# Order of loads, transposes and squares at the start of a hybrid decoder layer, with the pools of its last phase and the branch rows reordered

## The chip, the cores and the metric

The kernel runs on one NeuronCore of a Trainium2 chip. Its engines are TensorE (PE in the profile, with weight loads as PEld), VectorE (DVE), ScalarE (ACT), GpSimd (POOL) and SyncE (SP), which issues most of the transfers. The metric is the time of one execution on the device in microseconds; the profile belongs to one further execution.

## The reference

One layer of a decoder trunk is computed in float32 for a prompt of 1024 rows and for eight samples of 8 rows, together 1088 rows of width 1024. The weights are shared.

```
mod = silu(c) @ ada_w + ada_b;  shift, scale, gate = split(mod, 3)
h = rmsnorm(x, norm_g) * (1 + scale) + shift
z = h @ w_in + b_in                       # split into the inputs of A, B, C and the gates m_g
ya = chunk_gmlp(...)   * silu(a_g)        # A: mixing matrices over 128 positions
yb = swa_branch(...)   * silu(b_g)        # B: attention with a window of 128
yc = mlstm_branch(...) * silu(c_g)        # C: causal conv on q/k, matrix memory
merged = sum over branches of sigmoid(m_g) * (y @ w_branch)
x_out = x + gate * (merged @ w_out)
```

## The kernel before

Float32 products are made of three fast matmuls: each operand is split into a high part (rounded by a cast on ACT or DVE) and a low part (a subtraction on DVE), and high x high, high x low and low x high are added in one bank of PSUM. The rows stand in the free dimension, in three chunks `CH` of 384, 384 and 320 columns for `h` transposed, or in nine row tiles of 128 (the last has 64) for products by rows.

**The start** (up to about 87 us) loads x in nine tiles `xt` (x0 to x8), computes the modulation and makes `h` transposed, split into `hh[k]` and `hlo[k]` for k = 0 to 7. While it does so, the first weight slab is multiplied with it. `LOADS` gives the order of the transfers on SP: `x` a tile of x, `r` small rows, `a0` to `a3` the four parts of the modulation weights (four transfers of 512 KB each), `w0`, `w1` the halves of slab 0, `s` small rows. `STEPS` gives the order of the work, and inside it PE, ACT, DVE and POOL each keep that order (`manual_schedule`, line 451). The steps are:

- `Qn` (`squares`): ACT squares tile n and sums its rows; two small operations on POOL make the reciprocal root. `Nn` (`norm`): DVE scales tile n by it.
- `Tk c` (`x_keep`): PE transposes piece k of the chunk's three tiles into a bank of the pool `pss` (three banks, `pk`), and DVE or ACT copies it to SBUF. `place` puts the pieces into `xT0`, the first of the two slab buffers, and then into the slots m0, m1, ... of x tiles that are done.
- `Aj` (`mod_a`): 32 matmuls of modulation part j, and a copy on ACT. `Bj` (`mod_b`): eight small matmuls and four small operations on DVE, which leave scale and shift for k = 2j and 2j + 1.
- `Wi` (`slab0_split`): two casts on ACT, two subtractions on DVE. `Hk c` (`hprep`): ACT applies scale and shift, DVE makes the high and the low part, from the kept piece or, where `T` was not called, straight from the transposes in PSUM. `Gk c i` (`part`): three matmuls of slab half i with the piece, or six without i. `S`, `P` and `X` are small rows, the splitting of slab 1, and pads.

**The middle** (to about 598 us) goes through slabs 1 to 16, which alternate between the two buffers `hl` of the pool `wts`, and computes the conv, the matrix memory, the attention and the inner products of branch A. Outside the start a planner decides each engine's and queue's order by its own idea of when things are ready.

**The last phase** runs over a list of `items`. Each item has weights to prepare (`raw_load` on SP into one of five tiles `raw2`, `w_split` on ACT and DVE into a tile `prod`) and products of 288 and 256 columns (`CUT`). The first ones are the gate products of branch A; then come, for each branch, `gate_pair` and `proj`, where `proj` multiplies the branch's rows `yh`, `yl` by `w_branch` (`lastev` and the rest of `run`, lines 1698 to 1719). The rows of the second and third branch come from DRAM by `y_load`, whose item stands four items ahead of the branch's first `proj`. It goes through one tile `stage` with two halves:

```
for f in range(4):
    y_tiles(f)
    for b in range(2):
        c = slice(HT * b, HT * b + HT)
        x = stage[0][:, b]
        nc.sync.dma_start(x, dy[0 if br == 2 else 1, f, :, c])
        S.copy(yh[f][:, c], x)
        V.tensor_tensor(yl[f][:, c], x, yh[f][:, c].bitcast(F32), ALU.subtract)
```

`run` of `proj` multiplies the first 544 columns (h = 0) with k = 0 to 3 before the second 544.

The pools of the last phase lie where the pools `wts` and `gtmp` lay: first `e2` (14,336 bytes a partition: results and rows), then `w3` (6,144: sums of weights), then `w2` (10,240 for the five raw tiles and 24,576 for the six `prod`). In `wts` the two slab buffers have 16,896 bytes each.

Of the kernel before, what the change touches and what calls it, by code (L numbers as in the profile page):

```python
# [8 lines left out]
F32 = mybir.dt.float32  # L9
# [18 lines left out]
HT = NT // 2  # L28
HC = HT // 2
CUT = ((0, 288), (288, 256))  # L30
LEAD = 5
LOADS = "x0 r x1 x2 a0 x3 x4 x5 w0 x6 x7 x8 w1 a1 a2 a3 s"

STEPS = """Q0 N0 Q1 N1 Q2 N2
T20 T30 T40 A0 T50 T60 T70 Q3 B0 H00 H10 N3 Q4 N4 Q5 N5 W0
H01 H11 T21 T31 G000 G100 T41 T51 G010 G110 T61 T71 Q6 N6 Q7 N7 W1 Q8 N8
H02 H12 T22 G001 G101 T32 G011 G111 T42 T52 G020 T62 G120 T72 G021 G121
A1 B1 H20 H30 H21 H31 G20 G30 H22 G21 H32 G31 A2 G22 B2 G32 H40 H50 H41 H51 G40 G50 H42 G41 H52 A3 G51
B3 G42 H60 G52 H70 H61 H71 G60 H62 S G70 H72 P G61 G71 G62 G72 X"""


@with_exitstack
def trunk_kernel(ctx: ExitStack, tc: tile.TileContext, I, O):
    nc = tc.nc
    V, S, G, T = nc.vector, nc.scalar, nc.gpsimd, nc.tensor
# [32 lines left out]
    def slot(tag, shape, dt=F32, name=None):  # L78
        return sp.tile(shape, dt, tag=tag, name=name or tag)
# [16 lines left out]
    def kv(ap):  # L96
        return ap.rearrange("(k p) c -> p k c", p=128)
# [143 lines left out]
    with tc.tile_pool(name="start", bufs=1, side="right", reuse_waits="tile") as st:  # L241
# [47 lines left out]

        for step in LOADS.split():  # L290
            if step == "r":
# [82 lines left out]
        def place(n):  # L374
            if not places:
                places.append([xT0.rearrange("p a c -> p (a c)"), 0])
            if places[-1][1] + n > places[-1][0].shape[1]:
                places.append([slot(f"m{len(places) - 1}", [128, 1152], name="xT"), 0])
            p = places[-1]
            p[1] += n  # L380
            return p[0][:, p[1] - n:p[1]]

        def x_transpose(k, ci):
            px = pk()
            for i in range(3):
                t0, tn = TILES[3 * ci + i]
                tr(px[:, 128 * i:128 * i + tn], xt[3 * ci + i][:tn, 128 * k:128 * k + 128])
            return px

        def x_keep(k, ci):  # L390
            n = CH[ci][1]
            px = x_transpose(k, ci)
            kept_x[k, ci] = place(n)
            if k % 3:
                V.tensor_copy(kept_x[k, ci], px[:, :n])
            else:
                S.copy(kept_x[k, ci], px[:, :n])
# [37 lines left out]
        def start_step(step):  # L435
            d = [int(x) for x in step[1:]]
            if step == "P":
                load_pieces(1, [None] * 3 + [st.tile([128, 528], F32, name="raw1")])
            elif step == "S":
                ps = pk()  # L440
                tr(ps[:, 0:68], R1)
                V.tensor_copy(cols[:, 0:CADA], ps[:, 0:CADA])
                V.tensor_copy(cols[:, CCB:100], ps[:, CADA:68])
            elif step[0] == "G":
                for i in d[2:] or range(2):
                    part(d[0], d[1], i)
            else:
                {"Q": squares, "N": norm, "W": slab0_split, "A": mod_a, "B": mod_b, "T": x_keep, "H": hprep, "X": pads}[step[0]](*d)

        ET = mybir.EngineType  # L450
        with tc.manual_schedule(engines={ET.PE, ET.Activation, ET.DVE, ET.Pool}):
            for step in STEPS.split():
                start_step(step)
# [22 lines left out]
    with tc.tile_pool(name="cph", bufs=1, side="right", reuse_waits="tile") as c1:  # L476
# [303 lines left out]
        for h in range(1, 4):  # L780
            hl = next_slab()
            for s in range(2):
                f = 4 * s + h
# [616 lines left out]
    one.close()  # L1400


    e2 = ctx.enter_context(tc.tile_pool(name="e2", bufs=1, reuse_waits="tile"))
    w3 = ctx.enter_context(tc.tile_pool(name="w3", bufs=1, reuse_waits="tile"))
    w2 = ctx.enter_context(tc.tile_pool(name="w2", bufs=1, reuse_waits="tile"))
    banks = [0]

    def bank():
# [12 lines left out]
    newest = [None]  # L1421

    def raw_load(src):
        r = w2.tile([128, 512], F32, tag="raw", bufs=5, name="raw2")
        newest[0] = nc.sync.dma_start(r.rearrange("p (k c) -> p k c", k=src.shape[1]), src).ins
        return r

# [5 lines left out]
    def w_split(x, tile=None):  # L1433
        t = tile if tile is not None else w2.tile([128, 2, 512], F32R, tag="prod", bufs=6, name="prod")
        a = S.copy(t[:, 0], x)  # L1435
        b = V.tensor_tensor(t[:, 1], x, t[:, 0].bitcast(F32), ALU.subtract)  # L1436
        splits.append((a.ins, b.ins))
        return t
# [22 lines left out]
    def seven(cols2, order, final):  # L1461
# [4 lines left out]
        def loads():  # L1466
            for i, c in enumerate(cols2):
                w = kv(w_in[:, c:c + 128])
                for j in range(2):
                    st["a", i, j] = raw_load(w[:, 4 * j:4 * j + 4])  # L1470
# [95 lines left out]
    def plain(cols2, final):  # L1566

        st = {}

        def prep(i, j):  # L1570
            if not i and not j:
                return first[0]
            return w_split(raw_load(kv(w_in[:, cols2[i]:cols2[i] + 128])[:, 4 * j:4 * j + 4]))

        def run(i, h):
            for j in range(2):
                c = part_(h, j)
                ps = bank()[:, :CUT[j][1]]
                for k in range(8):
                    three(ps, st[i, k // 4], k % 4, hh[k][:, c], hlo[k][:, c], k == 0, k == 7)  # L1580
                x = tt(j)
                with tc.high_priority():
                    S.copy(x, ps)
                final(i, h, j, x)

        def have(i, j, t):
            st[i, j] = t
            if j:
                run(i, 1)

        out = [(lambda i=i, j=j: prep(i, j), lambda t, i=i, j=j: have(i, j, t)) for i in range(2) for j in range(2)]
        return out + [(None, lambda _, i=i: run(i, 0)) for i in range(2)]

    Q7 = (1, 6, 7, 5, 3, 2, 4)
# [29 lines left out]
    def y_tiles(f):  # L1624
        yh[f] = y2[0].tile([128, NT], F32R, tag=f"yh{f}", name="yh")
        yl[f] = slot(("y2", "y3", "y7")[f - 1], [128, NT], F32R, name="yl") if f else y2[0].tile([128, NT], F32R, tag="yl0", name="yl")
# [39 lines left out]
    def y_load(n):  # L1666
        br = ORDER_BR[n]
        if not stage:
            stage.append(slot("m5", [128, 2, HT], name="stage"))
        for f in range(4):  # L1670
            y_tiles(f)
            for b in range(2):
                c = slice(HT * b, HT * b + HT)
                x = stage[0][:, b]
                nc.sync.dma_start(x, dy[0 if br == 2 else 1, f, :, c])
                S.copy(yh[f][:, c], x)  # L1676
                V.tensor_tensor(yl[f][:, c], x, yh[f][:, c].bitcast(F32), ALU.subtract)
# [14 lines left out]
    def proj(n, f, Tt):  # L1692
        br = ORDER_BR[n]

        def prep():
            return w_split(raw_load(kv(I["w_branch_" + "abc"[br]][0][:, 128 * f:128 * f + 128])))

        def run(t):
            if n == 2 and f % 4 == 3:
                m_tiles(f)  # L1700
            for h in range(2):
                for j in range(2):
                    c = part_(h, j)
                    x = Tt[f, h, j]
                    ps = bank()[:, :CUT[j][1]]
                    for k in range(4):
                        three(ps, t, k, yh[k][:, c], yl[k][:, c], k == 0, k == 3)
                    prev = None
                    if n:
                        prev = mp(CUT[j][1], "mprev")  # L1710
                        lastm[0] = nc.sync.dma_start(prev, dmg[f, :, c]).ins
                    with tc.high_priority():
                        lastev[0] = V.scalar_tensor_tensor(x, x, 1.0, ps, ALU.add, ALU.mult).ins
                    if n:
                        V.tensor_tensor(x, x, prev, ALU.add)
                    if n == 2 and f % 4 == 3:
                        m_split(f, c.start, CUT[j][1], x)
                    else:
                        nc.sync.dma_start(dmg[f, :, c], x)

        items.append((prep, run))
# [106 lines left out]
    def wo_load(i):  # L1828
        for j in range(4):
            t = None  # L1830
            if SLOTS[i]:
                t = slot(SLOTS[i][j], [128, 1040], F32R, name="wo")[:, 16:1040].rearrange("p (a c) -> p a c", a=2)
            a = KS8[2 * j]
            src = kv(w_out[:, 256 * i:256 * i + 256])
            r = w2.tile([128, 512], F32, tag="raw", bufs=5, name="raw2")
            for u in range(2):
                nc.sync.dma_start(r[:, 256 * u:256 * u + 256], src[:, KS8[2 * j + u]])
            wo[i, j] = w_split(r, t)

    wo_load(0)  # L1840
    for i in range(4):
# [3 lines left out]
        c = slice(256 * i, 256 * i + 256)  # L1845
        for n in tuple(range(9)) if i < 3 else (8,) + tuple(range(8)):
# [4 lines left out]
            for z in range(8):  # L1851
                w, k = wo[i, z // 2], KS8[z]
# [50 lines left out]
```

## Time and profile before

| what | value |
|---|---|
| median of 3 runs | 1199.02 us (1198.87 to 1199.79) |
| profiled execution | 1201.82 us, span of its instructions 1200.1 us |
| PE busy | 1161.1 us, 97% of the span |
| DVE busy | 789.1 us, 66% |
| ACT busy | 490.2 us, 41% |
| POOL busy | 76.2 us, 6% |
| mean granted PE clock | 0.987 of full |

Busy time counts an instruction from its start to its end; matmuls overlap in the pipeline, so the pitch of a group says more than one's duration. "Idle before" is the time an engine stood still ahead of an instruction, with what ended it. The granted clock (PEclk) is a share of TensorE's full clock; 0.50 is its lower level. A window's row gives the stretch, its length, the busy time of PE, PEld, DVE, ACT and POOL in this order (with the number of instructions), PEclk, the busy share of the DMA engines and GB/s.

### The profile page before, as it was taken

What the parts mean: (1) busy time and instruction counts of PE and PEld (TensorE: products, weight loads), DVE (VectorE), ACT (ScalarE), POOL (GpSimd) and SP (SyncE); (2) the same over time, 40 slices, a digit from 0 to 9 for tenths busy, and PEclk for the clock granted to TensorE, in tenths of its full rate; (3) what the DMA queues carried; (4) which work ended last, traced back from release to release, by engine and by line L of the source; (5) the groups of instructions that cost most, each with busy time, mean ns of one, the idle gap of its engine ahead of it and who ended that gap; (6) DMA issues with size and microseconds to landing.
All of it is one profiled execution on the core that took longest, in us unless ns stands there. A gap on an engine that the chain in (4) does not pass through costs nothing.

```text
span 1200.1 us, 23137 instructions
## 1 busy us (share of the span) xinstructions
PE 1161.1 (97%) x8924; PEld 1115.8 (93%) x8924; DVE 789.1 (66%) x1862; ACT 490.2 (41%) x1233; POOL 76.2 (6%) x109
## 2 busy tenths in 40 slices
PE   4799999999999999999999999999999999999998
PEld 3589999999999998988998999999899999999998
DVE  4468768664549578886588975555666676668433
ACT  4343454543333367887354442223333342235100
POOL 2100002010114101020000000000000000000000
PEclk8799999999999999999999999999899999999999
DMA  9702223131323211122144225444533354455422
GB/s 299 241 23 77 73 63 109 31 106 64 109 65 94 61 33 58 54 67 78 40 133 143 63 72 161 145 131 143 166 110 110 110 169 128 128 183 187 135 90 74
DMA packets 150773, 129.74 MB, mean 108 GB/s; under 512 B 13613, under 2 KB 140213, under 8 KB 150648
## 3 DMA queue, kind: packets, MB, share of 16 engines
q1 hardware_dynamic: 142984, 118.96, 33.7%
q0 software_dynamic: 2240, 7.08, 1.7%
q10 hardware_dynamic: 5440, 2.23, 0.7%
q8 instruction: 70, 1.15, 0.4%
q14 instruction: 39, 0.32, 0.1%
HBM read 99.39 MB, written 29.82 MB: 108 GB/s over the span
## 4 chain that ended last, share of the span: by engine, by line
PE 85%; DVE 7%; DMA 3%; ACT 2%; issue 1%; POOL 0%; SPq 0%; DVEq 0%; ACTq 0%; POOLq 0%
PE pg L89 45%; PE pk L89 24%; PE pu L89 13%; PE pk L93 2%; DMA stage<-dy 1%; DVE hl L129 1%; DVE acc L494 1%; PE pu L93 1%; DMA raw<-in_w_in_dram 1%; DMA xt<-in_x_prompt_dram 0%; DVE vv L535 0%; DMA Cs<-in_state_mlstm_C_dram 0%; ACT junk L332 0%; DMA E<-scr 0%; DMA dy<-stage 0%
## 5 line engine op out<-in xcount | busy, mean ns | idle before, releaser
L89 PE MATMUL pg<-hl,hl 128*128 128x256 f32 (+3 forms) x904 | 277.9, 308 | 0.5 <-DVE hl L414 0.3
L89 PE MATMUL pg<-hh,hl 128*128 128x384 f32 (+1 forms) x912 | 238.7, 336 | 2.7 <-DVE hh L413 2.7
L89 PE MATMUL pg<-hl,hh 128*128 128x256 f32 (+1 forms) x1008 | 177.2, 283 | 0.2 <-DVE zif L539 0.2
L89 PEld LDWEIGHTS pg<-hl,hl 128*128 128x128 f32 x904 | 171.1, 189 | 2.0 <-DVE hl L414 1.2
L89 PEld LDWEIGHTS pg<-hh,hl 128*128 128x128 f32 x912 | 163.1, 190 | 5.8 <-DVE hh L413 3.5
L89 PEld LDWEIGHTS pg<-hl,hh 128*128 128x128 f32 x1008 | 150.4, 188 | 0.7 <-PE pg L89 0.4
L1435 ACT CAST prod<-raw 128x512 fp32r<-128x512 f32 x76 | 47.0, 620 | 127.9 <-PE pk L89 55.7
L89 PE MATMUL pg<-hh,prod 128*128 128x288 f32 (+1 forms) x400 | 84.0, 290 | 2.3 <-ACT prod L1435 2.1
L89 PE MATMUL pk<-hh,prod 128*128 128x256 f32 (+1 forms) x384 | 78.3, 285 | 0.0
L1436 DVE TENSOR_TENSOR prod<-raw,prod 128x512 fp32r<-128x512 f32 x76 | 52.0, 687 | 29.4 <-ACT prod L1435 29.1
L89 PEld LDWEIGHTS pg<-hh,prod 128*128 128x128 f32 x400 | 65.8, 188 | 3.2 <-ACT prod L1435 2.3
L1435 ACT CAST prod<-comb 128x512 fp32r<-128x512 f32 x60 | 36.9, 616 | 68.8 <-PE pk L89 30.9
L1599 ACT ACTIVATE tt<-tt,bh 128x288 f32<-128x288 f32 x96 | 49.9, 522 | 36.9 <-DVE tt L1561 14.2
L89 PEld LDWEIGHTS pk<-hh,prod 128*128 128x128 f32 x384 | 62.9, 189 | 0.8 <-DVE hl L840 0.4
L89 PE MATMUL pg<-yh,prod 128*128 128x288 f32 (+1 forms) x288 | 61.9, 293 | 0.0
L89 PE MATMUL pk<-yh,prod 128*128 128x256 f32 (+1 forms) x288 | 59.4, 286 | 2.3 <-ACT yh L1676 2.3
L89 PE MATMUL pg<-hl,prod 128*128 128x288 f32 (+1 forms) x200 | 57.7, 289 | 0.0
L89 PE MATMUL pk<-tc,prod 128*128 128x256 f32 (+1 forms) x408 | 56.3, 287 | 0.0
L89 PE MATMUL pu<-hh,prod 128*128 128x288 f32 (+1 forms) x272 | 56.3, 287 | 0.0
L89 PE MATMUL pg<-tc,prod 128*128 128x288 f32 (+1 forms) x396 | 55.8, 290 | 0.0
L89 PE MATMUL pk<-hl,prod 128*128 128x256 f32 (+1 forms) x192 | 54.7, 285 | 0.0
L89 PEld LDWEIGHTS pk<-tc,prod 128*128 128x128 f32 x408 | 52.7, 188 | 1.3 <-issue 1.3
(542 smaller groups left out, 2657.6 us busy)
## 6 DMA issues: line engine op xcount, KB each, us to landing
raw<-in_w_in_dram SPq DMA_DIRECT2D x124, 256.0 KB
adaraw<-in_ada_w_dram SPq DMA_DIRECT2D x16, 512.0 KB
stage<-dy SPq DMA_DIRECT2D x24, 272.0 KB
dmg<-tt SPq DMA_DIRECT2D x44, 144.0 KB
dmg<-tt SPq DMA_DIRECT2D x44, 128.0 KB
mprev<-dmg SPq DMA_DIRECT2D x32, 144.0 KB
xt<-in_x_prompt_dram SPq DMA_DIRECT2D x8, 512.0 KB
graw<-in_ada_w_dram SPq DMA_DIRECT2D x16, 256.0 KB
```

Of the source, the lines that this page charges most:

```text
L89: T.matmul(out, lhsT=lhsT, rhs=rhs, start=start, stop=stop)
L93: T.transpose(out, in_, ident[:k, :k])
L129: V.tensor_tensor(hl[:, 1, off:off + m], raw[:, :m], hl[:, 0, off:off + m].bitcast(F32), ALU.subtract)
L494: V.scalar_tensor_tensor(acc, xp[:, j:j + XC], cwcol[:, 8 * j + f:8 * j + f + 1], acc, ALU.mult, ALU.add)
L1435: a = S.copy(t[:, 0], x)
L1436: b = V.tensor_tensor(t[:, 1], x, t[:, 0].bitcast(F32), ALU.subtract)
L1599: S.activation(x, x, AF.Tanh, bias=bh[:, b:b + 1], scale=0.5)
```

## The change

The nine x tiles are loaded before all modulation weights and slab halves. `STEPS` is written anew: all 24 transposed pieces are kept (18 before), all of them are made before the first `H`, squares stand about one tile ahead of the scaling, and each pair A, B stands between the products of the pair before. In the last third of the columns the kept pieces alternate between ACT and DVE. The raw tiles get a pool of their own, `w2r`, and the pools of the last phase are opened as w2r, w3, e2, w2. `y_load` claims all four tiles first and then goes through the four tiles for the first half of the columns and then for the second.

```diff
--- before.py
+++ after.py
@@ -29,14 +29,13 @@
 HC = HT // 2
 CUT = ((0, 288), (288, 256))
 LEAD = 5
-LOADS = "x0 r x1 x2 a0 x3 x4 x5 w0 x6 x7 x8 w1 a1 a2 a3 s"
-
-STEPS = """Q0 N0 Q1 N1 Q2 N2
-T20 T30 T40 A0 T50 T60 T70 Q3 B0 H00 H10 N3 Q4 N4 Q5 N5 W0
-H01 H11 T21 T31 G000 G100 T41 T51 G010 G110 T61 T71 Q6 N6 Q7 N7 W1 Q8 N8
-H02 H12 T22 G001 G101 T32 G011 G111 T42 T52 G020 T62 G120 T72 G021 G121
-A1 B1 H20 H30 H21 H31 G20 G30 H22 G21 H32 G31 A2 G22 B2 G32 H40 H50 H41 H51 G40 G50 H42 G41 H52 A3 G51
-B3 G42 H60 G52 H70 H61 H71 G60 H62 S G70 H72 P G61 G71 G62 G72 X"""
+LOADS = "x0 r x1 x2 x3 x4 x5 x6 x7 x8 a0 w0 a1 w1 a2 a3 s"
+
+STEPS = """Q0 N0 Q1 N1 Q2 N2 Q3 T00 T10 T20 Q4 N3 T30 T40 Q5 T50 N4 T60 T70
+Q6 N5 T01 T11 Q7 N6 T21 T31 T41 Q8 N7 T51 T61 N8 T71 T02 T12 T22 A0 T32 T42 W0 T52 T62 B0 T72
+H00 H10 G000 H01 G100 H11 G010 H02 G110 H12 A1 G020 G120 B1 W1 G001 G101 G011 H20 G111 H30 G021 H21 G121
+H31 G20 H22 G30 H32 A2 G21 B2 G31 G22 H40 H50 G32 H41 H51 G40 H42 G50 H52 G41 A3 G51 B3 G42
+H60 H70 G52 H61 H71 G60 H62 S G70 H72 G61 P G71 G62 G72 X"""
 
 
 @with_exitstack
@@ -391,7 +390,7 @@
             n = CH[ci][1]
             px = x_transpose(k, ci)
             kept_x[k, ci] = place(n)
-            if k % 3:
+            if k % (2 if ci == 2 else 3):
                 V.tensor_copy(kept_x[k, ci], px[:, :n])
             else:
                 S.copy(kept_x[k, ci], px[:, :n])
@@ -1400,9 +1399,7 @@
     one.close()
 
 
-    e2 = ctx.enter_context(tc.tile_pool(name="e2", bufs=1, reuse_waits="tile"))
-    w3 = ctx.enter_context(tc.tile_pool(name="w3", bufs=1, reuse_waits="tile"))
-    w2 = ctx.enter_context(tc.tile_pool(name="w2", bufs=1, reuse_waits="tile"))
+    w2r, w3, e2, w2 = (ctx.enter_context(tc.tile_pool(name=n, bufs=1, reuse_waits="tile")) for n in ("w2r", "w3", "e2", "w2"))
     banks = [0]
 
     def bank():
@@ -1421,7 +1418,7 @@
     newest = [None]
 
     def raw_load(src):
-        r = w2.tile([128, 512], F32, tag="raw", bufs=5, name="raw2")
+        r = w2r.tile([128, 512], F32, tag="raw", bufs=5, name="raw2")
         newest[0] = nc.sync.dma_start(r.rearrange("p (k c) -> p k c", k=src.shape[1]), src).ins
         return r
 
@@ -1669,8 +1666,9 @@
             stage.append(slot("m5", [128, 2, HT], name="stage"))
         for f in range(4):
             y_tiles(f)
-            for b in range(2):
-                c = slice(HT * b, HT * b + HT)
+        for b in range(2):
+            c = slice(HT * b, HT * b + HT)
+            for f in range(4):
                 x = stage[0][:, b]
                 nc.sync.dma_start(x, dy[0 if br == 2 else 1, f, :, c])
                 S.copy(yh[f][:, c], x)
@@ -1832,7 +1830,7 @@
                 t = slot(SLOTS[i][j], [128, 1040], F32R, name="wo")[:, 16:1040].rearrange("p (a c) -> p a c", a=2)
             a = KS8[2 * j]
             src = kv(w_out[:, 256 * i:256 * i + 256])
-            r = w2.tile([128, 512], F32, tag="raw", bufs=5, name="raw2")
+            r = w2r.tile([128, 512], F32, tag="raw", bufs=5, name="raw2")
             for u in range(2):
                 nc.sync.dma_start(r[:, 256 * u:256 * u + 256], src[:, KS8[2 * j + u]])
             wo[i, j] = w_split(r, t)
```

## Rows read from the trace of the kernel before

**Rows 1.** Windows of the start: length, busy us per engine, PEclk, DMA share, GB/s.
```profile
12.30:40.00 27.70, 16.26 (x102) 12.14 (x102) 15.83 (x36) 13.59 (x25) 6.29 (x12) 0.83 1.09 339
40.00:56.90 16.90, 14.55 (x87) 10.62 (x87) 6.57 (x21) 3.75 (x7) 0.00 (x0) 0.78 0.69 218
56.90:87.00 30.10, 27.95 (x197) 23.90 (x198) 20.27 (x68) 13.43 (x25) 0.00 (x0) 0.94 0.01 3
```

**Rows 2.** Waits of PE, 0 to 87 us: total us, times, longest.
```profile
PE pk L93 <- DVE xt L337: 14.1, 8, 3.1
```

**Rows 3.** Timeline of PE near 600 us: start, us, instruction, idle before.
```profile
601.73 0.40 PE L89 MATMUL pg<-hh,prod 128*128 128x288 f32 x1 [2.08 <-ACT prod L1435]
```

**Rows 4.** Timeline of SP's queue, 597 to 602 us.
```profile
597.99 2.58 SPq L1425 DMA_DIRECT2D raw<-in_w_in_dram  x5
```

**Rows 5.** Timeline of PE, near 850 us.
```profile
853.30 0.61 PE L89 MATMUL pk<-yh,prod 128*128 128x288 f32 x1 [2.33 <-ACT yh L1676]
```

**Rows 6.** Windows behind these two waits.
```profile
602.46:608.00 5.54, 5.54 (x32) 5.54 (x33) 4.16 (x7) 2.62 (x6) 0.54 (x1) 0.69 0.97 271
853.30:860.00 6.70, 6.54 (x28) 6.22 (x29) 3.40 (x7) 1.41 (x3) 0.00 (x0) 0.52 0.35 106
```

**Rows 7.** Chain that ended last, 0 to 120 us: start, us, what.
```profile
9.29 1.16 ACT junk L332 x2
...
10.90 0.56 POOL rstd L167
11.48 0.77 DVE xt L337
...
17.21 1.28 PE pk L93 x9
...
23.50 0.94 POOL rstd L167
...
42.18 2.22 PE pg L89 x6
...
62.24 0.52 PE pg L89 x3
...
63.29 1.86 PE pk L89 x32
...
75.97 0.81 PE pk L89 x8
```

**Rows 8.** Timeline of DVE, 37 to 62 us.
```profile
37.46 1.29 DVE L288 TENSOR_TENSOR hl<-raw,hl 128x512 fp32r<-128x512 f32 x2
...
56.46 0.36 DVE L413 CAST hh<-hf 128x384 fp32r<-128x384 f32 x1 [0.45 <-ACT hf L407]
...
57.33 0.35 DVE L413 CAST hh<-hf 128x384 fp32r<-128x384 f32 x1
...
59.92 0.22 DVE L410 TENSOR_TENSOR hf<-xT,modA 128x64 f32<-128x64 f32 x1
...
61.27 0.22 DVE L410 TENSOR_TENSOR hf<-xT,modA 128x64 f32<-128x64 f32 x1
```

**Rows 9.** Timeline of PE, last matmul of the start's steps.
```profile
86.72 0.30 PE L89 MATMUL pk<-hh,hl 128*128 128x320 f32 x1
```

**Rows 10.** Timeline of SP's queue, 818 to 862 us.
```profile
830.87 0.42 SPq L1675 DMA_DIRECT2D stage<-dy  x1
...
832.59 0.32 SPq L1675 DMA_DIRECT2D stage<-dy  x1
...
846.74 0.32 SPq L1675 DMA_DIRECT2D stage<-dy  x1
...
848.34 6.02 SPq L1675 DMA_DIRECT2D stage<-dy  x3
```

**Rows 11.** Timeline of ACT, 846 to 862 us.
```profile
849.66 0.65 ACT L1676 CAST yh<-stage 128x544 fp32r<-128x544 f32 x1 [1.40 <-DMA stage<-dy]
...
852.61 0.65 ACT L1676 CAST yh<-stage 128x544 fp32r<-128x544 f32 x1 [0.54 <-DMA stage<-dy]
```

## The prediction

> **What bounds the kernel now.** I began with the table of busy time: TensorE (PE) is busy 97% of the span, so an edit counts only if it gives PE back time in which it waits, or in which its clock is low. Then I looked where those 3% lie. The windows of the first 87 us [rows 1] show PE busy 16.3 of 27.7 us and 14.6 of 16.9, at granted clocks of 0.83 and 0.78, then 28.0 of 30.1 at 0.94. Look also at DMA in them: full (share 1.09, 339 GB/s) until 40 us, next to nothing after 57. The waits say for whom PE stood: 14.1 us in eight waits for a scaled x tile [rows 2]. From that I read the cause: modulation weights (a0, 2 MB) and the slab's w0 are queued between x2 and x6, so the squares of x3 to x8 come late, and the engines run in the written order of steps, so PE can't go on with other work.
>
> Behind the start there are two more places. PE waits 2.08 us, to 601.73, for the first product weights of the last phase [rows 3]: SP sent their raw loads only at 597.99 [rows 4]. It waits 2.33 us, to 853.30, for yh [rows 5]. Behind each the granted clock is low for a while: mean 0.69 over 5.54 us, 0.52 over 6.70 us [rows 6].
>
> **The start, step by step.** No arithmetic is removed. Six more transposed pieces are copied to SBUF (24 where it was 18; k = 0 and 1 were read from PSUM before). PE does the same 24 transposes, 48 matmul groups (one step G has one or two) and four pairs A, B. The loads are the same bytes and the same issues in another order, so the queue's end is unmoved. A tile is 512 KiB, 1.5 us at 339 GB/s [rows 1]; x2 is there by 9.3, as its square starts then [rows 7]; x3 to x7 follow by 16.8, the half tile x8 by 17.5. Four loads of 0.5 MB (a0) take 6 us and w0 1.5: a0 23.5, w0 25, a1 31, w1 32.5, a2 38.5, a3 44.5.
>
> ACT: a square takes 1.16 [rows 7]. After Q2 (10.45) come six squares, 7.0 us, five copies between them at some 0.45 (estimate: DVE's 384-column copy bounds it, inside a pitch of 0.87 for two operations [rows 8]), 2.2, and waits for the first transposes and for DVE's scalings, about 2.2: Q8 ends at 21.9, after its tile has come, so ACT and not DMA sets this. From a square's end to the scaling it was 1.0 (10.45 to 11.48) [rows 7]; one POOL step took 0.94 instead of 0.56 when DVE scaled beside it, and here N7 does run beside Q8's: 1.4, then 0.77 for N8: 24.1.
>
> By this row one POOL step is 0.4 longer, and that is in the 24.1. The Trainium skill, "SBUF — State Buffer", section "Who interferes with whom", goes further: GpSimd and VectorE in some of its operations take a shared port in turn, and the second waits in full. By it both of POOL's steps could each stand behind a scaling of 0.77, which is 1.1 more than by the row: the start would save 15.9 and not the 17.0 below. The rows show one step held, not two, so I stay with them.
>
> Then PE: three transposes for each piece, 1.28 for nine [rows 7], so 0.43. T02, T12, T22 1.3; A0 1.86 at the high clock, 2.6 taken, as PE has been half idle; T32 to T62 1.7; B0 0.81, 1.1 taken; its four small operations on DVE 0.65 (estimate); H00 0.66 on ACT (estimate: a little over a DVE operation on the same piece) and 0.4 for DVE's cast [rows 8]. W0 (1.29 on DVE [rows 8]) falls beside the transposes. Sum 8.4: first G at 32.5. The written order of before comes to its first G behind fewer transposes and no x3; here the change loses some us.
>
> From there PE has everything it needs close by. A group of three 384-column matmuls takes 0.52 at the high clock (2.4 GHz) and 1.11 at the low (1.2 GHz; 2.22 for two) [rows 7]; with 320 columns 0.44, by the share of the columns. 32 x 0.52 + 16 x 0.44 = 23.7. A1 to A3 3 x 1.86 = 5.6, B1 to B3 3 x 0.81 = 2.4, S 0.4: 32.1 us. On top: the first groups at the low clock, about 2.5 (four groups at 1.11 - 0.52 = 0.59 more); G001 behind W1, whose subtraction (1.29) stands on DVE behind B1's scalings, 1.3; small waits on H in the first pair, 1.2. Sum 5. Last G: 32.5 + 32.1 + 5 = 69.6, against 87.0 now [rows 9]. Is DVE in front? Each H costs it 0.87 (start to start of two casts), 1.35 for the last third [rows 8]: 3.09 per k, 24.7 for eight, with W1, three B's and S 28.3, so 60.8 without waits: PE decides. A1 (36.6), A2 (47) and A3 (57) start behind their loads (31, 38.5, 44.5). The copy of the six extra pieces, about 1.4 on each of ACT and DVE, stands in that 24.1; H reads SBUF at the same 0.87.
>
> Saving 17.4, less 0.4 (estimate) of the next product that now runs inside the last G's: 17.0. Bounds: if all 5 us of losses vanish and A0 runs at 1.86, 23; if G starts 3 us later and two pairs run at the low clock, 7.
>
> What follows (slab 1's split, the conv, the token products) is ordered as before and moves as a whole; its loads are asked for when buffers come free, so they move along.
>
> **The pools.** By my sum over the pools' sizes the raw loads of the last phase lay 20 to 30 KB above the bottom of the space that the slabs leave, in the second slab buffer, which the last slab holds to the end. Now they lie at the bottom, in the first buffer, which holds the slab before it. So the five loads can go while PE still works on the last slab, and split and cast come before PE runs dry (601.73 - 2.08 = 599.65). Saved: 2.08, and the low clock behind it, 5.54 x 0.31 = 1.7: 3.8. Bounds: 0, if the bottom is held as long; 3.8. I take 3.8, the upper end: SP has five loads waiting there that nothing else in the code holds back, and it starts them 1.66 before PE runs dry, which fits a buffer held by PE's last slab. The other pools only change neighbours.
>
> **Branch rows by halves.** Each branch takes eight loads through two stage halves. Written by halves, four loads in a row use one stage half, each behind the subtraction of the one before. If SP kept that order, the second half would start only behind the fourth load. But SP's order isn't the code's: the row of 848.34 holds three, of which, counting from 830.87, only one is this branch's eighth [rows 10]; the other two belong to the next branch and went by 854.4, before this branch's products were done. A load whose stage half is free goes out, so the two chains should still interleave as now (830.87, 832.59 [rows 10]). Does it help then? PE, free at 850.97, started at 853.30, just behind the cast of 852.61, by its place the last tile's other half; the cast of the half that it reads, at 849.66, was over by 850.31 [rows 11]. So the wait goes by the whole tile here, and halves in order give nothing: I take 0. Bounds: minus 2.33 + 6.70 x 0.48 = 5.5 (wait and low clock gone), plus what the serial rival costs.
>
> **Sum.** 17.0 + 3.8 = 20.8. Span 1200.1 to 1179.3, the profiled execution's 1201.8 to 1181.0. The median of the runs is 2.8 below the profiled one, and I move it by the same: 1199.0 to **1178.2 us**.
>
> **Rivals.** (a) The yh wait goes as well: 1178.2 - 5.5 = 1172.7. For it: the first half's four loads stand first wherever engines choose. Against: the whole-tile wait.
> (b) The wait at 599.65 stays: 1182.0. For it: I inferred the addresses; no row shows them. Against: the 597.99 above.
> (c) The start stays at the low clock through k = 0 and 1: twelve groups, 8 x 0.59 + 4 x 0.5 = 6.7, and A1 1.3 more, 8 together: 1186.2. For it: groups are fed at 0.87 or slower in the first pair, so PE has holes; 0.83 and 0.78 in [rows 1]. Against: at the low clock a group (1.11) is longer than DVE's 0.87, so it has no holes there. The Trainium skill, "TensorE: Matmul & The Clock Gate", section "HAM oscillation — how this bites in real kernels", warns of just this: gaps between bursts bring the half clock back. The 0.52 behind the yh wait agrees: a wait of 2.33 was followed by it.
> (d) Slower: SP keeps the written order of the branch loads. A turn is (846.74 - 830.87) / 3 = 5.29 us [rows 10]. The second half's fourth load would go at 846.74 + 0.4 + 3 x 5.29 = 863.0, be landed and cast 3.57 later (846.74 to 850.31) at 866.6 instead of 853.3: 13.3 us, in two branches 26.6: 1204.8. It decides once both together cost over 20.8. Against: SP's reordering above; the second branch also has slack now.
> (e) The order of the start gains nothing because something I don't see comes late: about 1195 to 1199.
>
> **How the numbers follow.** Forecast 0.58; (a) 0.13; (b) 0.09; (c) 0.12; (d) 0.05; (e) 0.03. A measurement tells some 0.2% (2.4 us) from no change. Faster 0.93, same 0.02, slower 0.05. From (a) with 3 us of a better start to (c) with 3 us of a worse one: 1169 to 1189; outside lie (d), (e) and bad ends of the start's bound, under 2 in 10.
>
> **What would show it.** Right: the squares end near 22 us; first G near 32.5, last near 70; PE clock full from about 45 us; no wait for xt after 25 us; raw loads of the last phase sent before 598 and no wait on the first products. The yh wait tells (a) from the forecast, and SP's order of the eight loads tells (d). Wrong: last G after 80 us, PE waiting there for modulation weights or H; new waits of several us at the branch loads.

## The result and the profile after

The changed kernel takes 1185.04 us, the median of 1184.53, 1185.04 and 1186.71; a fourth run took 1608.58 at a mean granted clock of 0.656 and is not compared (with it the median would be 1185.88). The kernel before took 1199.4 beside it, 1198.87 to 1201.35. The ratio is 0.988 with an interval of 0.986 to 0.990: faster, by some 14 us where 20.8 were forecast, inside the range. The profiled execution took 1185.04, its span is 1183.3, 16.8 shorter than before's.

Windows of the start in the trace after (columns as in [rows 1]):

```profile
12.00:28.00 16.00, 11.97 (x75) 9.46 (x79) 10.53 (x19) 9.90 (x20) 7.02 (x14) 0.89 1.09 327
28.00:36.00 8.00, 5.61 (x41) 3.52 (x33) 4.22 (x17) 3.62 (x8) 0.00 (x0) 0.84 1.11 337
36.00:40.00 4.00, 4.00 (x12) 3.55 (x12) 3.73 (x11) 2.25 (x5) 0.00 (x0) 0.50 1.10 348
40.00:46.00 6.00, 5.00 (x52) 3.45 (x51) 4.40 (x12) 2.95 (x6) 0.00 (x0) 0.98 0.86 272
46.00:75.00 29.00, 28.18 (x216) 24.91 (x215) 21.13 (x72) 13.84 (x26) 0.00 (x0) 1.00 0.24 77
```

From 46 us on PE is busy 28.18 of 29 us at the full clock. The holes of [rows 1] now nearly all lie ahead of 46 us: in the first 36 us, 1.0 us just ahead of 45.56, and, at the low clock, the first products. The waits of PE in the same trace:

```profile
PE pk L92 <- DVE xt L336: 8.0, 5, 2.4
PE pk L88 <- ACT yh L1674: 3.3, 1, 3.3
PE pk L88 <- DVE cols L360: 1.5, 1, 1.5
PE pg L88 <- DVE hl L287: 1.0, 1, 1.0
PE pk L92 <- DVE xts L336: 0.8, 1, 0.8
```

The 14.1 us for x [rows 2] are 8.0, none of them past 20 us; the wait for the last, half tile (`xts`), 0.8 where it was 1.9, ends at 25.57. The wait for a small copy on DVE (`cols`) has grown to 1.5 from 0.6, and the 1.0 for slab 0's second half is new. Where they stand is in the timeline of PE after, from modulation part A0 on (the last line answers to [rows 9]):

```profile
26.92 1.93 PE L88 MATMUL pk<-adaraw,sT 128*32 128x256 f32 x32
...
31.07 0.24 PE L92 MATMUL pk<-ident,Ra 32*128 32x32 f32 x1
32.86 1.41 PE L88 MATMUL pk<-sel,msb 128*128 128x9 f32 x8 [1.54 <-DVE cols L360]
...
35.93 0.69 PE L88 MATMUL pg<-hh,hl 128*128 128x384 f32 x1 [0.85 <-DVE hh L412]
...
74.32 0.31 PE L88 MATMUL pk<-hh,hl 128*128 128x320 f32 x1
```

The start's last matmul starts at 74.32 and not at 86.72: 12.4 us earlier. What DVE did ahead of that copy, in its timeline:

```profile
31.01 1.29 DVE L287 TENSOR_TENSOR hl<-raw,hl 128x512 fp32r<-128x512 f32 x2 [1.06 <-ACT hl L286]
32.22 0.48 DVE L394 COPY xT<-pk 128x320 f32<-128x320 f32 x1
32.62 0.18 DVE L360 COPY cols<-pk 128x32 f32<-128x32 f32 x1
```

W0's subtraction (1.29) and the copy of T52 stand in front of it, and all of PE's next steps behind it.

In the last phase, SP's queue (it answers to [rows 4]) and the first products of PE (to [rows 3]):

```profile
551.55 36.79 SPq L1422 DMA_DIRECT2D raw<-in_w_in_dram  x7
```

```profile
586.66 0.40 PE L88 MATMUL pg<-hh,prod 128*128 128x288 f32 x1
...
587.39 0.53 PE L88 MATMUL pg<-hh,prod 128*128 128x288 f32 x2 [0.20 <-DVE prod L1433]
```

The raw loads begin 35 us ahead of the first product, and the fifth of them goes 18 us ahead of it (568.95). The wait of 2.08 is gone; a wait of 0.20 for DVE behind the first two matmuls was there before as well. The last product of the last slab stands 12.98 us earlier than before (584.67 for 597.65), one behind the boundary 16.68 (591.56 for 608.24): 3.7 us come from here. At the branch rows PE and ACT show (as [rows 5] and [rows 11]):

```profile
837.59 0.40 PE L88 MATMUL pk<-yh,prod 128*128 128x288 f32 x1 [3.28 <-ACT yh L1674]
```

```profile
834.08 0.64 ACT L1674 CAST yh<-stage 128x544 fp32r<-128x544 f32 x1 [2.19 <-DMA stage<-dy]
...
836.89 0.65 ACT L1674 CAST yh<-stage 128x544 fp32r<-128x544 f32 x1 [0.41 <-DMA stage<-dy]
```

The wait is there as before, 3.28 for 2.33, and again it ends behind the last of the eight casts. SP's loads still come in pairs for the two stage halves (814.23 and 815.96, the eighth from 831.98), so the written order of four by four isn't kept.

### The profile page after: what moved, and what is told of

It is laid out like the page before. It is cut to its first block, busy times and chain, and to the rows that moved or that the text cites. A ratio compares the mean times of both kernels' runs of the same rounds, so it can differ in the third digit from the quotient of the medians.

```text
span 1183.3 us, 23152 instructions
## 1 busy us (share of the span) xinstructions
PE 1154.0 (98%) x8924; PEld 1111.0 (94%) x8924; DVE 787.9 (67%) x1864; ACT 491.1 (41%) x1237; POOL 75.0 (6%) x109
## 4 chain that ended last, share of the span: by engine, by line
PE 87%; DVE 6%; DMA 3%; ACT 2%; issue 1%; SPq 0%; POOL 0%; ACTq 0%; DVEq 0%
PE pg L88 46%; PE pk L88 24%; PE pu L88 14%; PE pk L92 2%; DMA stage<-dy 1%; DVE hl L128 1%; PE pu L92 1%; DVE acc L493 1%; DMA raw<-in_w_in_dram 1%; DMA xt<-in_x_prompt_dram 1%; DVE vv L534 0%; DMA Cs<-in_state_mlstm_C_dram 0%; DMA dy<-stage 0%; ACT junk L331 0%; DVE yl L1675 0%
```

## The experiments

Times are medians; of a kernel that ran once, its one time. Runs of one kernel spread over up to 6 us (1196.43 to 1202.4 for the kernel before), so a single run doesn't tell a difference of 2 or 3 us. The kernel before took 1199.2 to 1201.8 beside them.

**Each part alone.** Three kernels, each the kernel before with one part of the diff: the first two hunks (start), the pools, the loop order of `y_load`.

> The kernel before with only the new order of loads and steps (and the alternation of copies in the last third of the columns). Theory: the three parts add up, and the start's part is what the two traces show between the last G's, 87.0 - 74.6 = 12.4 us, not the 17.0 that I forecast: about 1186.5 to 1187 us where before has 1199.2, a ratio near 0.9895, with the waits at the first products of the last phase (2.1) and at yh (2.3) still there. Rival: the start alone gives the 13.5 to 14 us of the whole change, and the other two parts nothing: 1185 us, 0.988.

> The kernel before with only the pools of the last phase in the new order. Theory: the wait of 2.08 us and the low clock behind it go, 3.8 us: 1195.4 us, ratio 0.997; the raw loads go out before 597 us. Rival: the loads went out early in the changed kernel only because its earlier start shifted something; then the wait stays and the time is 1199.2.

> The kernel before with only the branch rows by halves. Theory: the two chains of loads still interleave and PE still waits for the whole tile, so the time stays within 1.5 us of 1199.2; the wait for yh is 2 to 4 us, as in the changed kernel (3.3). Rival: with the start unmoved the order by halves does take the wait away: 1193.7.

Start alone: 1185.06 (1182.77 to 1187.72), ratio 0.988 (0.986 to 0.990); the last matmul of the start at 73.08. Pools alone: 1197.26, ratio 0.9978 (0.9967 to 0.9988), 2.7 us; raw loads from 563.80 on. Halves alone: 1200.35, ratio 1.0004 (0.9994 to 1.0014), nothing. So the start is nearly all of it, and the halves are nothing. Start and pools together should give 17.6 and gave 14.4; either is known to 1 to 3 us, and one thing in the windows of the start alone shows why the sum is loose:

```profile
585.00:590.00 5.00, 2.64 (x18) 2.40 (x19) 2.68 (x5) 3.42 (x7) 0.54 (x1) 1.00 1.04 291
590.00:595.00 5.00, 5.00 (x42) 5.00 (x41) 3.21 (x6) 0.99 (x3) 0.00 (x0) 1.00 0.99 291
```

PE waits 2.3 us for the first products here, as before, but the clock behind the wait stays at 1.00, where it was 0.69 in [rows 6]. With the halves alone it is the same: a wait of 2.0 us, and 1.00 in the windows behind it. The 1.7 us that I counted for the clock are there in one execution and not in two others.

**SP in written order** (one run), the price of the slower rival:

```diff
+        chain = [newest[0]]
...
-                nc.sync.dma_start(x, dy[...])
+                with tc.issue_after(chain[0]):
+                    chain[0] = nc.sync.dma_start(x, dy[...]).ins
```

> The changed kernel, with an edge on SP's queue from each of a branch's eight loads to the next, so that they go out in the written order. This prices the rival (d) of the prediction. By its sum: 13 us of wait at the first branch and up to as much at the second, a time of 1198 to 1211 us where the changed kernel has 1185; the second half's first load goes out behind the first half's fourth. Rival: the second branch has enough slack and other loads held behind the chain do no harm: 1190 or less.

1199.65 us, 14.6 more than the changed kernel. PE's waits for the branch rows in this run:

```profile
PE pg L88 <- ACT yh L1676: 7.9, 4, 2.7
PE pk L88 <- ACT yh L1676: 2.8, 1, 2.8
```

The mechanism is real and costs about half of the 26.6 that I gave it: with 0.9 for yl, 11.6 us of waits, and low clock behind them (0.50 to 0.54 from 835 to 855). All of them stand at the first of the two branches, for which I had 13.3; the second has no wait for yh. The change isn't that slow only because SP doesn't keep the order of the code.

**Loads and steps apart** (one run each): the changed kernel with the old `LOADS`, and with the old `STEPS`.

> The changed kernel with the old order of loads, all other edits kept. Theory (the new order of the work inside the start carries most of the gain, the loads only the part by which x8 lands later): with a0 (2 MB) and w0 (0.5 MB) ahead of the last x tiles, x8 lands about 2.5 MB later, some 7.5 us at 339 GB/s, near 25 us instead of 17.5; squares and scalings then end near 28 instead of 25.5, the first G comes near 38 instead of 35.9 and the last start-step near 76.5 to 77 instead of 74.6: 1187 to 1189 us. Rival (the loads carry the gain, as the forecast read the cause): PE waits for x tiles as before, some 10 us or more in all, the last G is past 83 us and the time 1194 or more.

> The changed kernel with the old STEPS (18 kept pieces, old alternation of the copies), the new order of loads kept. Theory: the old steps ask for A0 behind T40, and a0 now lands behind all x tiles, near 24 us; in the written order everything behind A0 waits for it, so A0 starts near 24 instead of 15, the first G is near 34 instead of 29, but no x tile is late any more behind it. The last G ends between 83 and 90 us, so the loads alone give back at most 4 us and may lose 3: 1194 to 1201 us. Rival (the loads carry the gain): last G near 75, 1187 us or less.

Old loads: 1194.85, last matmul of the start at 83.35; PE waits 6.6 us for x and 4.7 for ACT's copies of pieces, and A0 takes 3.64 instead of 1.93. Old steps: 1207.09, slower than before by 6.7, last matmul at 96.66. PE's waits in that run:

```profile
PE pk L93 <- DVE xt L337: 15.8, 8, 3.4
PE pk L89 <- DMA adaraw<-in_ada_w_dram: 6.6, 4, 5.4
```

Both theories missed; for the old loads the rival came out in place and time. Both kernels also have the new pools, worth 2.7 us by themselves, so what the start gains is read from its last matmul: at 87.5 with the old start (mean of three traces), at 73.7 with the new one (mean of six). The new steps on the old loads end it 4 us earlier; the new loads under the old steps end it 9 us later. Only together do they give 14: loading x first makes the modulation weights late, and only the new steps have work that doesn't need them.

**W0 earlier** (one run):

```diff
-... T12 T22 A0 T32 T42 W0 T52 T62 B0 T72
+... T12 T22 W0 A0 T32 T42 T52 T62 B0 T72
```

> The changed kernel with the split of w0 three steps earlier, ahead of A0. Theory: the 1.5 us in which PE waits for the small DVE copy in front of B0 come from W0's subtraction (1.29) and one copy ahead of it on DVE; with W0 earlier this wait falls under 0.4 and the first G comes 1.0 to 1.6 us earlier, counted from the last scaling (10.4 to 9.0 us or less). The last G and the end follow: about 1.3 us less, which one look can't tell by the time alone. Rival (w0 has not landed by then, and ACT's casts hold the copies of the transposes): the first G keeps its distance or moves later.

1183.71. In the timeline of PE:

```profile
26.41 2.77 PE L88 MATMUL pk<-adaraw,sT 128*32 128x256 f32 x32
...
31.95 1.06 PE L88 MATMUL pk<-sel,msb 128*128 128x9 f32 x8 [0.28 <-DVE cols L360]
...
34.65 0.45 PE L88 MATMUL pg<-hh,hl 128*128 128x384 f32 x1 [1.17 <-DVE hh L412]
```

The wait is 0.28, as the theory said, so W0's subtraction was its cause. But from the start of the last scaling (23.64) to the first product it is still 11.0 us, where it was 11.2: here the clock was low in A0 (mean 0.68), 0.84 longer, and in the three pieces transposed ahead of it, 0.6 longer, and the wait for hh grew from 0.85 to 1.17. The theory is right on the wait and not shown on the time.

**Branch rows without the stage:**

```diff
-                x = stage[0][:, b]
+                x = yl[f][:, c].bitcast(F32)
```

> The changed kernel with the branch rows loaded straight into the place of their low part, cast from there and subtracted in place, without the stage and its turns: the eight loads don't wait for each other. Theory (the chain of turns through two stage halves makes the rows late, and with the whole-tile wait it is the last of eight that counts): the loads all go when the first can, the wait of 3.3 us for yh and 0.4 for yl go, and the low clock behind them (about 1.2) with them: 1180 to 1183 us, 3 to 5.5 below the changed kernel. Rival (the tiles themselves come free late, not the stage): the loads go late all together, the wait stays over 2 us, and the time is 1185 to 1187.

1179.29 (1177.15 to 1181.2), ratio 0.983 (0.981 to 0.985), and a little below what was expected. It saves 21.1 us on the kernel before beside it where the changed kernel saves 14.4: 6.7 more. SP's queue:

```profile
809.69 0.86 SPq L1673 DMA_DIRECT2D yl<-dy  x2
...
812.72 3.62 SPq L1673 DMA_DIRECT2D yl<-dy  x5
```

The first went at 808.81, and all eight are out by 816.34; with the stage the eighth went no earlier than 831.98. PE has no wait for yh, and the clock is 1.00 in every window from 800 to 850. The tiles were free; the turns through the stage made the rows late.

**Which half does PE wait for?** My forecast had PE wait for both halves of a tile. Two kernels test that. First (one run), the second halves loaded in reverse order:

```diff
-            for f in range(4):
+            for f in (range(4), range(3, -1, -1))[b]:
```

> The changed kernel with the second halves of the branch rows loaded in the order of tiles 3, 2, 1, 0, the first halves in the order 0 to 3 as before; only the order inside the second stage half changes. Theory (a product waits until both halves of the tile that it reads are written): the half that comes last now belongs to tile 0, so PE stops at the branch's first product and not ahead of its fourth group k = 3; the wait for yh is longer by the nine products and about 1.1 us that PE did before it, some 4.3 instead of 3.3 us, and it ends behind the cast of tile 0's second half. Rival (it waits for its own half only, and the cast of the other half stood ahead of the wait's end by chance): PE still stops at k = 3, behind the cast of tile 3's first half, and waits some 0.5 to 1 us.

1183.82. The casts on ACT, the last two of eight:

```profile
833.15 0.65 ACT L1674 CAST yh<-stage 128x544 fp32r<-128x544 f32 x1 [1.91 <-DMA stage<-dy]
...
835.46 0.63 ACT L1674 CAST yh<-stage 128x544 fp32r<-128x544 f32 x1
```

And PE, from the branch's first product on:

```profile
833.52 0.29 PE L88 MATMUL pk<-yh,prod 128*128 128x288 f32 x1
...
836.14 0.40 PE L88 MATMUL pk<-yh,prod 128*128 128x288 f32 x1 [1.26 <-ACT yh L1674]
```

In this order the last casts are tile 0's second half and tile 3's first, whichever goes first. PE reads tile 0 at 833.52, before either is over (833.80 and 836.09). So it doesn't wait for the other half: my theory falls, and the cast that PE waits for is tile 3's first half, which comes last. The new theory was that the first halves run second because their stage half comes free later. The next kernel exchanges the stage halves and gives the two casts lines of their own (`row` issues a load, a cast by the function given, and a subtraction):

```diff
+        for f in range(4):
+            row(stage[0][:, 1], f, 0, first)
+        for f in range(4):
+            row(stage[0][:, 0], f, 1, second)
```

> The changed kernel with the two halves of the stage exchanged: the first halves of the branch rows go through the stage half that comes free first, the second halves through the other; the casts of the two have lines of their own, so that the trace tells them apart. Theory (after the run with the second halves in another order: a product waits only for the half that it reads, and that half of the last tile is loaded last, because its stage half comes free later than the other): the last cast now is a second half, PE starts its group k = 3 right behind the cast of the last first half, one turn earlier; the wait for yh of 3.3 us falls to 0.3 to 1.5, and with the clock 2 to 4 us are saved: 1182 to 1184 us. Rival (the forecast's reading: a product waits for both halves of its tile): PE still starts behind the last cast of the eight, the wait stays at 2.5 us or more, 1185 to 1187.

1180.45 (1178.87 to 1181.92), ratio 0.984 (0.982 to 0.986): 19.8 us saved, 5.4 more than by the changed kernel. ACT, where L1676 casts first halves and L1679 second ones:

```profile
832.07 0.65 ACT L1676 CAST yh<-stage 128x544 fp32r<-128x544 f32 x1 [1.48 <-DMA stage<-dy]
835.21 0.65 ACT L1679 CAST yh<-stage 128x544 fp32r<-128x544 f32 x1 [0.74 <-DMA stage<-dy]
```

PE's fourth group, k = 3, and the next column piece behind it:

```profile
833.20 0.43 PE L88 MATMUL pk<-yh,prod 128*128 128x288 f32 x2
...
833.90 0.28 PE L88 MATMUL pu<-yh,prod 128*128 128x256 f32 x1
```

Now the first halves are ahead; PE runs through k = 3 at 833.2 without a wait, two us before the last cast even starts. That is the gain that "by halves" could have had.

**All of it.** Rows in place, `W0` ahead of `A0`, `W1` ahead of `A1`, and squares two tiles ahead of the scaling; then the same with B0 and the first two H between the last transposes:

```diff
-T30 T40 Q5 T50 N4 T60 T70 Q6 N5 T01 T11 Q7 N6 ...
+T30 T40 Q5 T50 N4 Q6 T60 T70 N5 Q7 T01 T11 N6 Q8 ...
-H02 G110 H12 A1 G020 G120 B1 W1 G001
+H02 G110 H12 W1 A1 G020 G120 B1 G001
...
-T22 W0 A0 T32 T42 T52 T62 B0 T72 H00 H10 G000
+T22 W0 A0 T32 T42 B0 T52 H00 T62 H10 T72 G000
```

> The branch rows in place, and three moves in the written order: the split of w0 ahead of A0, the split of w1 ahead of A1, the squares two tiles ahead of the scaling. Theory (the 3 us by which the start's saving fell short are waits that the order makes): the wait of 1.0 us for slab 0's second half goes, the wait of 1.5 for the small DVE copy ahead of B0 stays under 0.4, the last scaling comes about 1 us earlier than 22.6 to 24.8; the last G ends 2 to 3 us before the 72.4 to 74.3 of the kernels with the changed start, near 70 to 71, and the time is 2 us or a little more under the kernel with rows in place alone (1179.3): 1176.5 to 1178. Rival (the clock takes back what the waits give, as it did with w0 early alone, where A0 took 2.77 instead of 1.93): last G at 72 or later, time 1178.5 to 1180.

> As the kernel with all four edits, and B0 and the first two H moved between the transposes of the last third (B0 behind T42, the first H behind T52, the second behind T62), so that the chain from A0 to the first product (copy, B0, four small operations, ACT, DVE) runs while PE still transposes. Theory: the wait of about 1.2 us for hh goes and the low clock in the first groups (0.50 for some 2 to 4.5 us) is shorter; first G 1.5 us earlier by the distance from the last scaling (10.8 to 11.2 before, 9.3 to 9.7 now), last G 1 to 2 us earlier than with the four edits: 1175 to 1177. Rival (the copies of the remaining pieces stand behind the small operations on DVE and delay the first products as much): distance unchanged, time within 1 us of the kernel with four edits.

1175.08 (1174.55 to 1176.07), ratio 0.980 (0.978 to 0.981); and 1174.66 (1174.07 to 1175.44), the same ratio. The start's last matmul is at 70.76 and 69.90. The first is 4.2 us below the rows in place alone (3.0 when each is held against the kernel before beside it), more than was expected; the second isn't told apart from it, though its wait for hh is 0.16 and no longer 1.18. Both beat the changed kernel by 10 us. Windows of the second, with PE's waits of 0.28 (to 28.85) and 0.16 (to 32.02) in them and no others:

```profile
24.00:28.00 4.00, 4.00 (x44) 2.25 (x44) 2.04 (x7) 2.56 (x5) 0.00 (x0) 1.00 1.11 334
28.00:30.00 2.00, 1.72 (x14) 1.36 (x12) 1.02 (x5) 0.43 (x1) 0.00 (x0) 1.00 1.10 348
30.00:31.00 1.00, 1.00 (x7) 0.59 (x6) 1.00 (x5) 0.59 (x1) 0.00 (x0) 0.96 1.12 339
31.00:32.00 1.00, 0.86 (x3) 0.34 (x3) 0.51 (x5) 1.00 (x4) 0.00 (x0) 0.50 1.14 309
32.00:36.00 4.00, 3.98 (x11) 3.23 (x12) 3.80 (x10) 2.98 (x7) 0.00 (x0) 0.50 1.09 334
```

The clock falls to 0.50 at 31 us though PE was busy for all but 0.28 us from 24 on.

## Why the prediction came out 6.8 us low

The miss of 1185.04 - 1178.2 = 6.8 has two parts. The span was forecast at 1179.3 and is 1183.3: 4.0. And I moved the forecast 2.8 down from the profiled execution to the median; after, the profiled execution is the median: 2.8. That offset was spread between executions: later sets of the kernel before have medians of 1199.2 to 1200.4, and its profiled 1201.8 is among its slower runs. What I priced in such a run isn't all there to be saved in a usual one; the 1.7 us of low clock behind the wait of [rows 3] are a part of that kind.

**The start: the mechanism was right, the term was 3 to 4.6 us too large.** 17.0 forecast, 12.4 in this pair of traces. One pair isn't the whole: the last matmul of the old start is at 86.72 to 88.76 in three kernels (mean 87.5), of the new one at 72.36 to 74.91 in the six kernels that share it (mean 73.7), so 13.9. Where it went, by the steps of the sum:

- N8 done at 24.1: 25.5 in this trace (its scaling starts at 24.77), 23.3 to 25.5 in the six traces. The first squares move with the landing of the tiles (x2's square at 9.29 before, 10.64 after; 9.68 with the start alone, on the same order of loads), so I take that for spread and not for a wrong step. ACT, not DMA, sets the end of the squares, as forecast; they end at 23.7 here and at 21.6 to 23.1 in the others, for 21.9.
- From N8 to the first G 8.4: 10.4 (25.5 to 35.93), and 10.0 to 10.9 in the six. This is the step that failed, and its words are "W0 falls beside the transposes". I named the cover and didn't put it in DVE's order: the subtraction ends where the copy of `cols` should already be done, and PE stands 1.54. The four transposed pieces took 2.3 and not 1.7 besides; A0 ran at the high clock, 1.93, and gave 0.7 back. With the moves of the last two kernels the distance is 8.8 and 8.1; W0's move alone took the wait away and not the time, as the clock took it back.
- From the first G to the end of the last 37.1: 38.7 (35.93 to 74.63). The wait behind W1 was 1.0 (1.3 forecast). The clock was low from about 33.4, in B0, to about 40.3, through four groups as forecast, and full behind them: rival (c) did not come.
- DVE was not in front, and the A's did not wait for their loads: right.

In the last two kernels the last matmul ends at 71.06 and 70.20 where 69.6 was forecast: the missing us were waits in the order, not work left out of the sum. How they divide between the moves isn't shown.

A small part of the same term is POOL. Its two operations for a reciprocal root take 0.19 and 0.55 when undisturbed; after, in POOL's timeline and in that of DVE beside it:

```profile
15.94 1.02 POOL L166 TENSOR_TENSOR rstd<-ss,mhalf 128x1 f32<-128x1 f32 x1
17.59 0.70 POOL L165 TENSOR_SCALAR ss<-ss 128x1 f32<-128x1 f32 x1 [0.63 <-ACT junk L331]
...
23.81 0.30 POOL L165 TENSOR_SCALAR ss<-ss 128x1 f32<-128x1 f32 x1 [0.99 <-ACT junk L331]
24.19 0.55 POOL L166 TENSOR_TENSOR rstd<-ss,mhalf 128x1 f32<-128x1 f32 x1
```

```profile
17.50 0.74 DVE L336 TENSOR_SCALAR xt<-xt,rstd 128x1024 f32<-128x1024 f32 x1
...
23.31 0.75 DVE L336 TENSOR_SCALAR xt<-xt,rstd 128x1024 f32<-128x1024 f32 x1
```

Six steps of the start are stretched, by 0.11 to 0.56 (0.70 for 0.19 and 1.02 for 0.55 above); I had counted one, by 0.4, at the last tile. A first operation that begins beside a scaling ends 0.05 behind it: at 18.29 behind 18.24, at 24.11 behind 24.06. At the last tile that cost 0.11, and from its square's end (23.72) to its scaling (24.77) it was 1.05 where I had 1.4. The Trainium skill, "SBUF — State Buffer", section "Who interferes with whom", says that GpSimd and VectorE, in some of its operations, lock each other out of a shared port and that the second waits in full; the trace agrees, and what a step loses is the rest of the scaling beside it, less than the 0.75 of a whole one. As I had read that rule the start saved 15.9, which is nearer to what was measured, but the rule's extra us is not where the time went.

**The pools: right in the wait, not in the clock.** 3.8 forecast, 3.7 in this pair of traces, 2.7 (1.4 to 4.0) alone. The raw loads start 35 us ahead of their product, with the pools alone too; of (b) nothing is left. The wait's 2.1 went in every run with the new pools; the clock's 1.7 depends on the execution. That the loads now lie in the first slab buffer is still my sum over the sizes; no row shows an address.

**Branch rows by halves: the number was right, the reason wrong.** 0 forecast, 0 measured (alone: ratio 1.0004). I read [rows 11] as "the last tile's other half": the first stage half should go first, so the cast of 852.61 had to be the second half's. It was the first half's. The planner sends the load first whose stage half comes free first, and that is the other one: the step ahead writes its result to DRAM out of the first half. Where the written order forces the first load into that half, it goes 229.2 us behind the last phase's first product (585.57 to 814.81), as the second load of the changed kernel does (229.3), whose first goes 227.6 behind it. Of the casts, the run with exchanged stage halves shows the order by its two lines, and the run with the reversed order that PE reads a tile whose other half isn't written. Both are kernels with the new loop order; for the kernel before I infer the same from the same stage. So, by the code, the changed loop order changed nothing because in either order each stage half holds the same four loads in the same sequence, and the two chains interleave the same way. The interleaving was foreseen; that the wait stays was read from the wrong half, and there the 0 is luck. What I had as rival (a), 5.5 us, was to be had by exchanging the halves (5.4) or by dropping the stage (6.7). Of the wait itself the trace told a true thing, the last cast; which row it was the trace doesn't print, and I supplied it.

**Rivals.** (d) costs 14 to 15 and not 26.6 where it is forced, as only one branch pays; the change doesn't meet it. (e) is out. The time lies nearest to (c)'s 1186.2, but (c)'s mechanism isn't what made it: the low clock ended with the first four groups. Not foreseen was that the order of loads alone ends the start 9 us later: I read the cause in the loads, and it is the pair of loads and steps.

**The clock.** I priced a low clock behind each wait of 2 us and for four groups at the start. The first was there after the wait of [rows 3] and absent after the same wait in the start alone and in the halves alone. The low clock at the first products stayed even where their waits were gone. The Trainium skill, "TensorE: Matmul & The Clock Gate", section "HAM oscillation — how this bites in real kernels", tells of a matmul kernel whose waits for DMA between bursts, longer than the bursts, bring the half clock back. The windows from 24 to 36 us above show a fall without such a gap, with 0.28 us of waits since 24 and one of 0.49 just before, which that doesn't explain. What made it fall there stays open.

## What to carry to other kernels

When several small operations share an in-order engine, write the engine's own order out around each step that you cost at nothing: "it runs beside the transposes" was true for PE and false for DVE, where it stood in front of a 0.18 us copy that all the rest waited for. A wait's releaser tells which instruction came last, not which data it carried; where two instructions look alike in the trace, give them lines of their own before building on the one you think it is. And order of loads and order of work are one edit: here the new order of work alone ended the start 4 us earlier and the new loads alone 9 us later, and both together 14 earlier.

## What the runs showed of the hardware

- A tile of x of 512 KB, the third of x in the queue, had its square start at 9.12 us in one kernel and at 10.70 in another with the same issues ahead of it (rows in place, second halves reversed); the start's last matmul stood at 72.36 and 74.91.
- The mean granted clock was 0.69 behind a wait of 2.08 us in one execution and 1.00 behind waits of 2.26 and 2.02 at the same place in two others; and it fell to 0.50 at 31 us in a stretch in which PE had been busy for all but 0.28 us since 24.
- 32 small matmuls of modulation took 1.93 us at a granted clock of 1.00, 2.77 at 0.68 and 3.64 at 0.50.
